# A two-layer decoder trunk in float32: the second score matmul of attention branches A and B over 128 rows instead of 64

## The chip, the core and the metric

The kernel runs on one core of a Trainium2 chip. The metric is the device time of one execution in microseconds (us). Engines are named as in the profile: PE is TensorE's matmul, PEld its weight load, DVE is VectorE, ACT is ScalarE, POOL is GpSimd, SP is SyncE.

## What is computed

Two layers of a decoder trunk on 512 tokens of width 1024. Per layer, h = RMSNorm(x), one input projection feeds three causal mixers, their outputs are gated and merged, then follow an output projection with a residual and a SwiGLU FFN with another. Branch A has 8 heads of width 64, branch B has 4 heads with two score maps each (differential attention), branch C has 8 heads of width 96 for the scores. The part that matters here:

```
scores of A: sc = q @ k.T * 64**-0.5 + bias_a[distance]        # q, k: 512 x 64 per head
scores of B: sc_i = q_i @ k_i.T * 64**-0.5 + bias_b[distance]  # i = 0, 1
p = softmax(masked sc)
```

## The kernel before

**Float32 by parts.** Every operand of a product is split into a hi part (rounded to fp32r) and a lo part (what is left), and a product is hi\*hi + hi\*lo + lo\*hi, three fp32r matmuls into one PSUM bank (`mm3`, line 264). The dense work (projections, gates, FFN) streams weights in units of up to 128x512: SP loads them, ACT makes the hi part (`_hi`, line 221), DVE the lo part (`_lo`, line 227).

**Scores of A and B.** Rows of a tile are SBUF partitions. `q_tile` (line 639) and `k_tile` (line 653) each turn one projection tile of 128 rows, two heads of 64 rows, into operands. For q, each head gets one tile that holds its hi part in its own 64 rows and its lo part in the other 64. For k, each head gets a tile with its hi part in both row halves (ACT writes one half at line 659, POOL copies it to the other at line 663), and both heads share a third tile, `k[2]`, with the lo parts, one in each half (DVE, line 662). `qk_stacked` (line 667) then makes one block of scores from two matmuls into one PSUM bank: the first runs over all 128 rows (hi of q and lo of q against hi of k), the second over the 64 rows of the head (hi of q against lo of k). A block is 128 queries by n keys, where n = 128, 256, 384, 512 for the four query blocks. A layer has 16 such score maps (8 heads of A, two for each of 4 heads of B), so 64 blocks, and the two layers have 128 such pairs of matmuls. Branch C uses `qk_plain` (line 675): three matmuls over 96 rows per block.

**Behind the scores.** `score_block` (line 693) adds the bias and takes the row maximum on DVE and the exponential on ACT; `scale_rows` (line 704) normalizes the rows on POOL; `transposed` (line 709) transposes the blocks on PE, and ACT and DVE split them for the product with v.

**Order.** The program is issued in a fixed order, in which each engine takes its own instructions one after the other. `weave` (line 363) makes that order: up to three threads of attention pieces (heads) run, and between them come steps of dense jobs. It decides by `Clock` (line 86), a rough model of every engine's time, in which a matmul costs by its columns alone (line 99) and a POOL operation on 512 columns about 0.66 us (line 105). A piece is issued when its inputs are ready by that model, else a dense step is. The k tiles of A and B are dense jobs (`qk_jobs`, line 680): in a layer the first tile of A stands ahead of the attention, the others among the jobs (lines 1074 to 1104). There are 16 k tiles in the two layers. All tiles of 128x512 come from one pool of 83 slots (`NSLOT`, line 30).

Of the kernel before, what the change touches and what calls it, by code (L numbers as in the profile page):

```python
# [9 lines left out]
F32 = mybir.dt.float32  # L10
F32R = mybir.dt.float32r
AF = mybir.ActivationFunctionType
ALU = mybir.AluOpType
# [5 lines left out]
P = 128  # L19
# [66 lines left out]
class Clock:  # L86
    """A rough clock of the engines while the program is traced. It only decides the order in
    which independent pieces are issued; Tile places every wait."""
    HOP = 0.18
# [74 lines left out]
class Kernel:  # L164
# [11 lines left out]

# [1 line left out]
    def slot(self, dt=F32):  # L178
# [23 lines left out]

# [1 line left out]
    def add_job(self, units, body, ready=None):  # L204
# [41 lines left out]
    def ahead(self, i, most=2):  # L246
        """loads and splits up to unit i and, a few at a time, beyond it"""
        n = len(self.units)
        ld, lh, ll = self.look
        self.load_ahead(min(n, i + 1 + ld))  # L250
        end = min(n, i + 1 + lh, max(i + 1, self.ph + most))
        while self.ph < end:
            self._hi(self.ph)
            self.ph += 1
        end = min(n, i + 1 + ll, max(i + 1, self.pl + most))
        while self.pl < end:
            self._lo(self.pl)
            self.pl += 1
# [3 lines left out]

# [1 line left out]
    def mm3(self, out, ah, al, bh, bl, first, last):  # L264
# [4 lines left out]

    def t_job(self, tiles, per_unit=4, halves=False, ready=None):  # L270
        """tiles: (wname, layer, [k-blocks], cols, rhs() -> [(hi, lo)], evac(psum));
        W block stationary, activations moving."""
        blocks = [(t, kb) for t in range(len(tiles)) for kb in range(len(tiles[t][2]))]
# [46 lines left out]
    def n_job(self, wname, layer, ks, cols, lhs, evac, groups=None, ready=None):  # L320
        """activations' token block stationary, W columns moving; evac(tb, psum)."""
        w = len(cols)
        units = [[(wname, layer, k, cols)] for k in ks]
        groups = groups or [1] * len(ks)

        def body(j):
            ps = None
            k0 = 0
            for g in groups:
                for tb in range(NT):  # L330
                    if g > 1 or tb == 0:
                        self.ahead(j.base + k0 + g - 1, 3)
                    if k0 == 0:
                        if ps is None:
                            ps = [None] * NT
                        ps[tb] = self.bank()
                    for kb in range(k0, k0 + g):
                        h, l = self.hi[j.base + kb], self.lo[j.base + kb]
                        ah, al = lhs(kb, tb)
                        o = ps[tb][:, :w]  # L340
                        mm = self.nc.tensor.matmul
                        mm(o, ah, h[:, :w], start=kb == 0, stop=False)
                        mm(o, ah, l[:, :w], start=False, stop=False)
                        mm(o, al, h[:, :w], start=False, stop=kb == len(ks) - 1)
                        if g > 1 and kb == k0 + g // 2 - 1:
                            yield
                    if k0 + g == len(ks):
                        evac(tb, ps[tb])
                    if g > 1 or tb == 1:
                        yield  # L350
                for kb in range(k0, k0 + g):
                    self.done(j.base + kb)
                k0 += g
                if g == 1:
                    yield

        return self.add_job(units, body, ready)
# [5 lines left out]
    def weave(self, threads, jobs):  # L363
        """Issues the threads' pieces as they come ready and dense steps in between.
        threads: list of (generator of readiness functions, group); a readiness function
        gives the time at which its piece can start, or None while that is unknown."""
        clock, free = self.clock, self.clock.free
# [41 lines left out]

# [1 line left out]
    def split(self, hi, lo, src, scale=None):  # L411
# [11 lines left out]

# [1 line left out]
    def rstd(self, parts):  # L425
        """parts: [P,1] shares of the mean square; -> (mean + eps) ** -0.5"""
        nc = self.nc
# [8 lines left out]
    def sumsq(self, src, out, n):  # L436
        """out = sum(src ** 2) / n"""
        self.nc.scalar.activation(self.junk[:, :src.shape[-1]], src, AF.Square, scale=n ** -0.5, accum_out=out)
# [10 lines left out]
    def norm_block(self, x, ss, g):  # L449
        """x: two halves of a token block -> normed halves (F32)."""  # L450
        nc = self.nc
# [46 lines left out]
def program(K):  # L498
# [26 lines left out]

# [1 line left out]
    bias_in = (K.slot(F32), [K.slot(F32) for _ in range(2)], [K.slot(F32) for _ in range(2)])  # L527
# [44 lines left out]
    def setup_bias():  # L572
        """bias of every distance, per head, and from it 128 rows to cut the strips from"""
        tab, oh, us = bias_in
# [23 lines left out]
def layer(K, l, plan, state, strip, C):  # L598
# [4 lines left out]

# [1 line left out]
    def norm1_stats(tb):  # L605
# [13 lines left out]

# [1 line left out]
    def v_evac(key, heads, hd):  # L621
        """token-major values as [hi | lo] per head, two slots per token block"""
        res = [None] * NT
# [13 lines left out]

# [1 line left out]
    def q_tile(key, off, m):  # L639
        """two heads of 64 rows; each gets one tile that stacks its hi and lo parts"""  # L640
        def evac(ps):
# [11 lines left out]
    def k_tile(key, off, m):  # L653
        """hi parts doubled over both row halves, lo parts of the two heads in one tile"""
        def evac(ps):
            k = [K.slot(F32R) for _ in range(3)]
            for i in range(2):
                a = slice(i * 64, i * 64 + 64)
                nc.scalar.copy(k[i][a], ps[a])
            for i in range(2):  # L660
                a, b = slice(i * 64, i * 64 + 64), slice(64 - i * 64, 128 - i * 64)
                nc.vector.tensor_tensor(k[2][a], ps[a], k[i][a], op=ALU.subtract)
                nc.gpsimd.tensor_scalar(k[i][b], k[i][a].bitcast(F32), 1.0, 1.0, op0=ALU.mult, op1=ALU.mult)
            V[key, m] = k
        return ("w_in", l, range(KD), rng(off + m * P, P), h, evac)

    def qk_stacked(q, k, i):
        rows = slice(i * 64, i * 64 + 64)

        def mm(out, qs, n):  # L670
            nc.tensor.matmul(out, q[i][:, qs], k[i][:, :n], start=True, stop=False)
            nc.tensor.matmul(out, q[i][rows, qs], k[2][rows, :n], start=False, stop=True)
        return mm
# [8 lines left out]

# [1 line left out]
    def when(keys, tiles, banks=0):  # L684
        """the time at which a piece can start; None before its inputs are issued"""
        def at():
# [22 lines left out]
    def transposed(ps):  # L709
        """P blocks -> per key block the (hi, lo) parts of its columns, queries from that block on"""  # L710
        pt = {}
# [19 lines left out]
    def head(hd, start, vkey, ykey, y):  # L731
        """one head of A or C: y[pair] collects the transposed outputs of two heads"""
        mm, ins, bias = yield from start(hd)
# [31 lines left out]

# [1 line left out]
    def start_a(hd):  # L767
# [5 lines left out]

# [1 line left out]
    def low_rank_evac(key, gi, w):  # L775
# [6 lines left out]
    def low_rank_q():  # L782
        """norm of cq and its transpose"""
        g = [K.slot(F32), K.slot(F32)]
# [24 lines left out]
    def low_rank_kv():  # L809
        """norm of ckv and its transpose; the rotary key, transposed"""  # L810
        g = K.slot(F32)
# [87 lines left out]

# [1 line left out]
    def head_b(hd, y):  # L901
# [65 lines left out]

# [1 line left out]
    BR = {"a": 0, "b": 1, "c": 2}  # L969
# [24 lines left out]

# [1 line left out]
    def residual_evac(hf, g_key):  # L996
# [17 lines left out]

# [1 line left out]
    V["ff"], V["m"] = {}, {}  # L1016
# [30 lines left out]

    # ======== jobs, in the order in which the tensor engine takes them ========
    def given(keys, tiles=lambda: []):
# [25 lines left out]
    jobs = []  # L1075
# [35 lines left out]
    def reload():  # L1111
        """the residual stream and the gain of the next norm"""
        src = ap["x"] if l == 0 else x_dram
# [20 lines left out]

    # ======== program ========
    def drain(jobs):
# [111 lines left out]
```

## Time and profile before

| | |
|---|---|
| three runs | 1924.22, 1925.93, 1927.16 us; median 1925.93 us |
| the profiled execution | known by its span, from the first to the last instruction: 1922.5 us, 3.4 us under the median |
| PE busy | 1895.5 us, 99% of the span |
| PEld, DVE, ACT, POOL busy | 82%, 48%, 42%, 12% |
| granted TensorE clock | 0.999 of full speed in the mean |

In the rows further down, a matmul or a weight load carries the rows and columns of the stationary operand and then the moving operand: `64*128 64x512` has 64 rows, 128 stationary columns and 512 moving columns. A timeline row merges neighbours of one kind and shows the first one's form. A matmul's own duration contains its way through the pipeline, so neighbours overlap; what a matmul takes of the engine is read from its start to the start of the next row. `<-issue` means that the engine waited for nothing that the profile shows.

### The profile page before, as it was taken

How to read it: one execution, taken by the hardware profiler on the slowest of the kernel's cores; microseconds unless marked ns; L12 is line 12 of the kernel's file. 1: busy time of each engine (PE TensorE's matmuls, PEld its weight loads, DVE VectorE, ACT ScalarE, POOL GpSimd, SP SyncE). 2: the span in 40 equal slices, each digit the busy share in tenths (PEclk: the TensorE clock that was granted, in tenths of full speed). 3: DMA queues.
4: the chain of work that ended last, by engine and by line, in shares of the span. 5: the costliest groups of instructions: out<-in, count | busy, mean ns of one | idle time of the engine just before them, and what ended most of it. 6: DMA issues, size and time to landing. Idle time of an engine off the chain costs nothing.

```text
span 1922.5 us, 25100 instructions
## 1 busy us (share of the span) xinstructions
PE 1895.5 (99%) x9148; PEld 1581.0 (82%) x9148; DVE 915.1 (48%) x1836; ACT 800.9 (42%) x1777; POOL 223.8 (12%) x405
## 2 busy tenths in 40 slices
PE   7999999999999999999999999999999999999998
PEld 5798988777888888888888888887878898888886
DVE  4556556556465333342354566565563553323331
ACT  4456655454344222232235656554443432323330
POOL 3222412111000000000002233211110000000000
PEclk9999999999999999999999999999999999999999
DMA  7422223224343322232423222132333332222321
GB/s 264 103 82 64 72 77 94 76 73 128 108 126 100 88 77 83 83 115 83 148 94 95 61 75 71 58 110 74 120 105 99 126 94 82 83 77 85 119 93 44
DMA packets 104604, 183.05 MB, mean 95 GB/s; under 512 B 13888, under 2 KB 24576, under 8 KB 104480
## 3 DMA queue, kind: packets, MB, share of 16 engines
q1 hardware_dynamic: 99216, 173.91, 29.4%
q0 software_dynamic: 3824, 4.91, 0.9%
q10 hardware_dynamic: 1440, 2.62, 0.4%
q8 instruction: 72, 1.18, 0.2%
q14 instruction: 52, 0.43, 0.1%
HBM read 177.15 MB, written 8.16 MB: 96 GB/s over the span
## 4 chain that ended last, share of the span: by engine, by line
PE 95%; DVE 2%; DMA 2%; ACT 1%; issue 0%; DVEq 0%; POOLq 0%; POOL 0%; ACTq 0%
PE d L154 83%; PE a L154 12%; DVE s L154 2%; ACT s L154 1%; DMA s<-in_x 1%; DMA s<-in_weights 1%; DMA s<-in_lambda_k 0%; DVEq L1237 0%; ACT junk L154 0%; DVE h L154 0%; POOLq L1237 0%; DVE gsub L154 0%; POOL m L154 0%; DVE lam L154 0%; DVE junk L154 0%
## 5 line engine op out<-in xcount | busy, mean ns | idle before, releaser
L154 PE MATMUL d<-h,s 128*128 128x512 f32 (+1 forms) x4224 | 947.8, 382 | 1.3 <-DVE s L154 1.3
L154 PEld LDWEIGHTS d<-h,s 128*128 128x128 f32 x4224 | 761.3, 188 | 151.3 <-issue 3.3
L154 PE MATMUL d<-s,s 128*128 128x512 f32 (+1 forms) x2400 | 548.3, 385 | 1.8 <-DVE s L154 1.8
L154 DVE TENSOR_TENSOR s<-s,s 128x512 fp32r<-128x512 f32 (+3 forms) x718 | 451.9, 669 | 184.1 <-ACT s L154 130.0
L154 PEld LDWEIGHTS d<-s,s 128*128 128x128 f32 x2400 | 443.3, 188 | 86.4 <-issue 3.6
L154 ACT CAST s<-s 128x512 fp32r<-128x512 f32 (+2 forms) x678 | 378.3, 603 | 278.0 <-DVE s L154 212.7
L154 PE MATMUL d<-s,h 128*128 128x512 f32 (+2 forms) x960 | 200.7, 358 | 7.7 <-DVE s L154 6.0
L154 PE MATMUL a<-s,s 128*128 128x256 f32 (+8 forms) x868 | 188.7, 332 | 8.9 <-DMA s<-in_c_onehot 8.9
L154 PEld LDWEIGHTS d<-s,h 128*128 128x128 f32 x960 | 162.9, 189 | 30.7 <-issue 8.8
L154 PEld LDWEIGHTS a<-s,s 128*128 128x128 f32 (+2 forms) x868 | 140.7, 188 | 53.7 <-issue 25.2
L154 DVE TENSOR_TENSOR s<-a,s 128x512 fp32r<-128x512 f32 (+5 forms) x196 | 111.5, 606 | 143.2 <-ACT s L154 142.6
L154 ACT ACTIVATE s<-s,m 128x128 f32<-128x128 f32 x192 | 107.7, 561 | 133.9 <-DVE m L154 132.3
L154 DVE TENSOR_TENSOR s<-d,s 64x512 fp32r<-64x512 f32 (+2 forms) x128 | 72.1, 587 | 170.6 <-PE d L154 110.7
L154 POOL TENSOR_SCALAR m<-m 128x1 f32<-128x1 f32 (+1 forms) x44 | 16.0, 363 | 1132.9 <-ACT junk L154 1132.7
L154 POOL TENSOR_SCALAR s<-s,m 128x128 f32<-128x128 f32 (+3 forms) x160 | 97.2, 625 | 426.9 <-DVE m L154 266.8
L154 DVE TENSOR_TENSOR s<-s,d 128x512 f32<-128x512 f32 x44 | 30.3, 688 | 226.8 <-PE d L154 226.8
L154 ACT ACTIVATE junk<-s 128x512 f32<-128x512 f32 (+3 forms) x96 | 47.0, 490 | 173.0 <-DVE s L154 167.2
L154 ACT ACTIVATE s<-d 128x512 f32<-128x512 f32 (+1 forms) x76 | 45.3, 596 | 148.4 <-PE d L154 148.2
L154 PE MATMUL a<-ident,s 128*128 128x128 f32 (+1 forms) x696 | 95.6, 278 | 0.0
L154 ACT CAST s<-a 128x512 fp32r<-128x512 f32 (+2 forms) x146 | 69.7, 534 | 59.8 <-PE a L154 59.1
L154 DVE CUSTOM_DVE_ANT_0 s<-a,s 128x128 f32<-128x128 f32 (+3 forms) x128 | 60.8, 489 | 68.5 <-PE a L154 68.1
L154 DVE SCALAR_TENSOR_TENSOR s<-s,m,s 128x512 f32<-128x512 f32 (+3 forms) x96 | 64.8, 713 | 58.3 <-POOL m L154 46.5
(48 smaller groups left out, 575.4 us busy)
## 6 DMA issues: line engine op xcount, KB each, us to landing
s<-in_weights SPq DMA_DIRECT2D x542, 256.0 KB, 2.7
s<-in_weights SPq DMA_DIRECT2D x56, 192.0 KB, 2.6
s<-u_rep SPq DMA_DIRECT2D x24, 256.0 KB, 2.7
s<-in_x SPq DMA_DIRECT2D x16, 256.0 KB, 5.9
s<-in_weights SPq DMA_DIRECT2D x16, 144.0 KB, 2.1
x_dram<-s ACTq DMA_DIRECT2D x8, 256.0 KB, 3.4
s<-x_dram SPq DMA_DIRECT2D x8, 256.0 KB, 5.4
out<-s SPq DMA_DIRECT2D x8, 256.0 KB, 2.0
```

The costliest lines, as they stand in the source:

```text
L154: return f(*args, **kw)
```

## The change

`k_tile` makes four tiles instead of three: the lo parts no longer share one tile, each head gets its own, in both row halves. The second half is a copy by POOL of what DVE wrote, two more POOL operations of 64x512 for each k tile, issued behind the two that copy the hi parts. The second matmul of a block runs over all 128 rows: the stationary operand is the same as that of the first (hi and lo of q), the moving operand is the doubled lo part of k. The block thereby also gets the product lo\*lo, which was left out before. The rest of the diff removes comments and docstrings.

```
     def k_tile(key, off, m):
         def evac(ps):
-            k = [K.slot(F32R) for _ in range(3)]
+            k = [K.slot(F32R) for _ in range(4)]
             for i in range(2):
                 a = slice(i * 64, i * 64 + 64)
                 nc.scalar.copy(k[i][a], ps[a])
             for i in range(2):
                 a, b = slice(i * 64, i * 64 + 64), slice(64 - i * 64, 128 - i * 64)
-                nc.vector.tensor_tensor(k[2][a], ps[a], k[i][a], op=ALU.subtract)
+                nc.vector.tensor_tensor(k[2 + i][a], ps[a], k[i][a], op=ALU.subtract)
                 nc.gpsimd.tensor_scalar(k[i][b], k[i][a].bitcast(F32), 1.0, 1.0, op0=ALU.mult, op1=ALU.mult)
+            for i in range(2):
+                a, b = slice(i * 64, i * 64 + 64), slice(64 - i * 64, 128 - i * 64)
+                nc.gpsimd.tensor_scalar(k[2 + i][b], k[2 + i][a].bitcast(F32), 1.0, 1.0, op0=ALU.mult, op1=ALU.mult)
             V[key, m] = k
...
     def qk_stacked(q, k, i):
-        rows = slice(i * 64, i * 64 + 64)
-
         def mm(out, qs, n):
             nc.tensor.matmul(out, q[i][:, qs], k[i][:, :n], start=True, stop=False)
-            nc.tensor.matmul(out, q[i][rows, qs], k[2][rows, :n], start=False, stop=True)
+            nc.tensor.matmul(out, q[i][:, qs], k[2 + i][:, :n], start=False, stop=True)
         return mm
```

## Rows read from the trace of the kernel before

**Rows 1.** The page, busy us of each engine (share of the span) and its instructions.
```profile
PE 1895.5 (99%) x9148; PEld 1581.0 (82%) x9148; DVE 915.1 (48%) x1836; ACT 800.9 (42%) x1777; POOL 223.8 (12%) x405
```

**Rows 2.** Busy by stretch, layer 0: A's later heads, then C's. Columns as its header.
```profile
core 0: us, PE busy (x) PEld busy (x) DVE busy (x) ACT busy (x) POOL busy (x), PEclk, DMA share, GB/s
...
143.00:188.00 45.00, 44.65 (x243) 36.71 (x244) 28.96 (x85) 27.13 (x72) 9.27 (x18) 1.00 0.23 65
188.00:339.00 151.00, 151.00 (x810) 132.41 (x809) 88.09 (x199) 87.28 (x197) 47.51 (x90) 1.00 0.26 81
```

**Rows 3.** Groups by form, PEld: busy, mean ns, then idle before them and its end.
```profile
L154 PEld LDWEIGHTS a<-s,s 96*128 96x128 f32 x192 | 31.3, 189 | 4.1
L154 PEld LDWEIGHTS a<-s,s 64*128 64x128 f32 x128 | 23.5, 184 | 26.2 <-issue 21.2 <-DVE s L154 0.4
```

**Rows 4.** Timeline of PE, layer 0, B's first head: start us, us, line, operation.
```profile
345.31 0.59 PE L154 MATMUL a<-s,s 128*128 128x256 f32 x2
345.83 1.66 PE L154 MATMUL d<-s,h 128*128 128x512 f32 x6
347.33 0.70 PE L154 MATMUL a<-s,s 128*128 128x384 f32 x2
347.96 1.66 PE L154 MATMUL d<-s,h 128*128 128x512 f32 x6
349.45 0.82 PE L154 MATMUL a<-s,s 128*128 128x512 f32 x2
350.20 2.12 PE L154 MATMUL d<-s,h 128*128 128x512 f32 x8
```

**Rows 5.** Timeline of PE, layer 0, one block of 128 columns of A.
```profile
81.64 0.48 PE L154 MATMUL a<-s,s 128*128 128x128 f32 x2
82.05 1.31 PE L154 MATMUL d<-s,h 128*128 128x384 f32 x6
```

**Rows 6.** Timeline of PE, layer 1, four blocks of B directly behind one another.
```profile
1403.32 2.69 PE L154 MATMUL a<-s,s 128*128 128x128 f32 x8
1405.95 1.66 PE L154 MATMUL d<-h,s 128*128 128x512 f32 x6
```

**Rows 7.** Timeline of PE, layer 0, blocks of C: three matmuls over 96 rows each.
```profile
227.27 0.86 PE L154 MATMUL a<-s,s 96*128 96x512 f32 x3
227.96 1.52 PE L154 MATMUL d<-h,s 128*128 128x512 f32 x6
...
236.10 0.69 PE L154 MATMUL a<-s,s 96*128 96x384 f32 x3
236.62 1.54 PE L154 MATMUL d<-h,s 128*128 128x512 f32 x6
...
254.52 0.45 PE L154 MATMUL a<-s,s 96*128 96x128 f32 x3
254.81 1.61 PE L154 MATMUL d<-h,s 128*128 128x512 f32 x6
256.26 0.52 PE L154 MATMUL a<-s,s 96*128 96x256 f32 x3
256.62 1.56 PE L154 MATMUL d<-h,s 128*128 128x512 f32 x6
```

**Rows 8.** Timeline, layer 0: making the first k tile of A, and its first scores.
```profile
55.69 1.32 POOL L154 TENSOR_SCALAR s<-s 64x512 fp32r<-64x512 f32 x2 [0.87 <-PE d L154]
56.17 1.41 DVE L154 TENSOR_TENSOR s<-d,s 64x512 fp32r<-64x512 f32 x2 [2.72 <-ACT s L154]
...
58.83 2.69 PE L154 MATMUL a<-s,s 128*128 128x128 f32 x8
```

**Rows 9.** Timeline, layer 0, PE's waits behind A's first heads; brackets: idle before, its end.
```profile
62.82 0.23 DVE L154 CUSTOM_DVE_ANT_0 junk<-s 128x64 f32<-128x64 f32 x1 [1.71 <-DMA s<-in_lambda_k]
...
64.86 2.56 PE L154 MATMUL d<-h,s 128*128 128x512 f32 x10 [1.28 <-DVE s L154]
...
76.51 0.76 PE L154 MATMUL d<-s,h 128*128 128x384 f32 x3 [2.85 <-DVE s L154]
```

**Rows 10.** Groups by form, POOL: the copies of hi parts; columns as in rows 3.
```profile
L154 POOL TENSOR_SCALAR s<-s 64x512 fp32r<-64x512 f32 x32 | 19.7, 616 | 87.9 <-ACT s L154 61.1 <-issue 14.2 <-PE a L154 10.4
```

More of the change, by code (lines that the diff above doesn't have):

```diff
@@ L655, in evac @@
         def evac(ps):
-            k = [K.slot(F32R) for _ in range(3)]
+            k = [K.slot(F32R) for _ in range(4)]
             for i in range(2):
@@ L661, in evac @@
                 a, b = slice(i * 64, i * 64 + 64), slice(64 - i * 64, 128 - i * 64)
-                nc.vector.tensor_tensor(k[2][a], ps[a], k[i][a], op=ALU.subtract)
+                nc.vector.tensor_tensor(k[2 + i][a], ps[a], k[i][a], op=ALU.subtract)
                 nc.gpsimd.tensor_scalar(k[i][b], k[i][a].bitcast(F32), 1.0, 1.0, op0=ALU.mult, op1=ALU.mult)
+            for i in range(2):
+                a, b = slice(i * 64, i * 64 + 64), slice(64 - i * 64, 128 - i * 64)
+                nc.gpsimd.tensor_scalar(k[2 + i][b], k[2 + i][a].bitcast(F32), 1.0, 1.0, op0=ALU.mult, op1=ALU.mult)
             V[key, m] = k
@@ L667, in qk_stacked @@
     def qk_stacked(q, k, i):
-        rows = slice(i * 64, i * 64 + 64)
         def mm(out, qs, n):
             nc.tensor.matmul(out, q[i][:, qs], k[i][:, :n], start=True, stop=False)
-            nc.tensor.matmul(out, q[i][rows, qs], k[2][rows, :n], start=False, stop=True)
+            nc.tensor.matmul(out, q[i][:, qs], k[2 + i][:, :n], start=False, stop=True)
         return mm
```

## The prediction

> **What bounds the kernel now.** I read the busy shares first. TensorE's matmul row is busy 99% of the span, the next compute engine 48% [rows 1]. A busy PE is not PE at its peak, so the question is how much of those 99% the touched matmuls hold without need.
>
> For that I went to the weight loads by form. 128 loads of 64 rows stand there, one for each second matmul of a score block in A and B, and ahead of them the load path sat idle 26.2 us, 21.2 of it for nothing that the profile shows. The 192 loads of 96 rows in branch C, which do the same kind of work, have 4.1 us [rows 3]. So a 64-row load is kept waiting, while its operand, the same q tile as that of the first matmul, is long there.
>
> The timeline of PE prices it. I take from the start of a pair to the start of what comes next. Standing alone between dense steps, a pair takes 0.52 us at 256 columns, 0.63 at 384 and 0.75 at 512 [rows 4], and 0.41 at 128 [rows 5]: 2.31 us for the four blocks of a map. Branch C is the comparison: there three matmuls over 96 rows, between the same dense steps, take 0.69 us at 512, 0.52 at 384, 0.36 at 256 and 0.29 at 128 [rows 7]. Two matmuls of A cost more than three of C. A switch between 128 rows and 64 rows, once into it and once out of it, is the one thing that A and B have and C lacks; 96 rows beside 128 cost nothing that is seen.
>
> Last I read the stretches, to see whether another engine would take over. In A's later stretch DVE is busy 28.96 of 45 us and ACT 27.13; in C's, where no such switch slows PE, DVE has 88.09 of 151 and ACT 87.28, and PE is busy without a break [rows 2]. At the pace without switches the other engines keep up.
>
> **The change, part by part.**
>
> *The second matmul over 128 rows.* It gets the form of its neighbours, so both switches of all 128 pairs go. Its price without them comes from C: a third of a block, 0.23, 0.173, 0.12 and 0.097 us [rows 7], so a pair costs two thirds: 0.46 + 0.35 + 0.24 + 0.19 = 1.24 us for four blocks. More rows add no columns, and 96 and 128 rows are both above the 64, so I take C's price as it stands. Against 2.31 us that saves 1.07 us per map; 32 maps give 34.2 us.
>
> That is the sum for pairs that stand alone. Pairs directly behind one another cost more: four of them take 2.63 us [rows 6], 0.32 over 2.31, so 0.107 for each of the three that follow another. In the timeline 52 of the 128 pairs follow another pair in this way (19 at 256 columns, 13 at 384, 13 at 512, 7 at 128). 52 x 0.107 = 5.6 us. Together **39.8 us** off PE. Bounds: 34.2 if only the stand-alone price goes, and 44.5 (32 x (2.63 - 1.24)) if all pairs cost as in rows 6.
>
> *What does not arrive.* Where PE waits for something that PE's pace doesn't move, the gain before it is lost. After the first heads of layer 0, PE waits 1.28 us and then 2.85 us for DVE [rows 9]. DVE's work there had been held up until 62.82 by the transfer of the lambdas [rows 9], which no matmul delays, and from there DVE and ACT follow one another closely. So what is won in the seven pairs ahead of the second wait only lengthens the waits: the first four, 2.63 - 1.24 = 1.39 us, and one each at 128, 256 and 384 columns, 1.56 us [rows 4, 5] and 0.1 for the one that follows another, less 0.78, 0.9 us. Together 2.3 us. I take that off: 37.5 us. In layer 1, the wait at the same place hangs on ACT's copy of a projection that PE itself ends, so it moves along; nothing is taken off there. Bounds: 0 to 4.6 (the same in both layers).
>
> *Two more POOL copies for each k tile.* 16 tiles x 2 x 0.616 us [rows 10] = 19.7 us on an engine that is busy 223.8 of 1922.5 us [rows 1]. The tightest place is the first head, whose scores start right behind its k tile: POOL's hi copies end at 57.01, DVE's two lo parts at about 56.88 and 57.58, and the first score starts at 58.83 [rows 8]. The new copies would run from 57.01 to 57.63 and from 57.58 to 58.20, 0.6 us ahead of the first score, and the second head, which uses the last copy, comes later. So they hide; without that cover, PE would wait 0.6 us or so at one tile. On POOL's queue, the scaling of an older head's rows may now stand behind two copies, 1.23 us; the order is planned with POOL's time in it, which puts a dense step in front of the transposes that wait. I take 0, bounds -1 to +10 us (half of 19.7).
>
> *DVE, ACT, DMA.* DVE writes the same two lo parts, to two tiles instead of one; counts and sizes stay. Nothing moves on SP. One more slot per k tile: counted from the code in issue order, at most 67 of the 83 slots are live while A and B make scores, and one or two more change nothing. 0 us.
>
> *The order.* `Clock` prices a matmul by its columns, so the plan's PE doesn't change, but two more POOL operations shift readiness times, and a few pieces will change places. PE's idle time behind the first 30 us is about 7 us, in eight gaps, of which rows 9 show the largest two. A changed plan can lose or add that much: 0, bounds -5 to +7.
>
> **The sum.** The span is 1922.5 us and the median of the runs 1925.93, 3.4 above; I keep that distance. 1922.5 - 37.5 + 3.4 = 1888.4 us. I predict **1888 us**, 2.0% under before.
>
> **The rivals.**
>
> *The load still waits.* What rows show: dense and 96-row loads run ahead of their matmuls without a wait, 64-row loads don't [rows 3]. Suppose instead that a load must wait wherever the previous matmul uses the same rows: then in the new pairs, which share all 128 rows, the second load would still stand behind the first matmul, and pairs would cost what they do now: 1926 us. Against it speaks rows 7, where three loads on the same 96 rows cost 0.23 us per 512-column matmul. This is also the case in which the change doesn't do what it says.
> The Trainium skill states such a rule (TensorE: Matmul & The Clock Gate, Part 3, The mechanism): a weight load overlaps a matmul in flight only where the row groups differ. By that rule nothing would be won; the trace disagrees, by the same rows 7 (0.23 us for each of three matmuls on the same rows).
>
> *Another engine takes a share.* A's heads run three at a time beside splits for projections; DVE is at 64% there [rows 2]. If half of A's share (64 of 128 pairs, 19.9 us) is lost in new waits for DVE, ACT or POOL, it is 1898 us; if all of it is, 1908. For it: PE already waits for DVE twice at A's start [rows 9]. Against it: C's stretch.
>
> *Slower: POOL becomes the way to the scores.* The copies of lo parts wait at the head of POOL's queue for DVE's subtractions. If at each of the 16 k tiles PE stood through both, 1.41 us for DVE's pair [rows 8] and 1.23 for two copies, that is 2.64 us a tile, 42 us in all: 1930 us. It decides from 37.5 / 16 = 2.35 us a tile. Against it: rows 8 leave some 0.6 us even at the tightest tile, and the other tiles are made long before their heads begin.
>
> **How the numbers follow.** The forecast as worked out (1881 to 1896) gets 0.84, another engine's share 0.09, the load that still waits 0.03, slower by POOL 0.04. The range is 1881 to 1899: below, the sum with 44.5 us and a plan that loses some waits; above, POOL's 10 us, or half of A's share gone. That leaves out the longer half of the second rival and the last two, and some of the forecast's own edges, between 1 and 2 in 10. A measurement of this kernel tells about 0.2% (3.9 us) from no change; faster 0.93, same 0.03, slower 0.04.
>
> **What would show it.** Right: no 64-row form is left in the groups; a stand-alone pair takes 0.46 us at 512 columns and 0.19 at 128; four in a row 1.24 and not 2.63; the loads of these blocks have the small idle time of the 96-row ones; PE's busy time falls by 38 to 40 us; the wait near 76 us in layer 0 grows by up to 2.3 us; POOL's busy time grows by about 20 us. Wrong: pairs that still take 0.7 us at 512 columns (the first rival), or pairs at 0.46 with new waits of PE for POOL or DVE around the heads (the others).

## The result, and the profile after

The changed kernel takes 1874.07 us (1873.35 to 1875.83, 4 runs), the kernel before 1925.08 beside it: a ratio of 0.9738, interval 0.9724 to 0.9752, so 51.0 us or 2.6% less. The prediction was 1888 us with a range of 1881 to 1899: the right way and the right mechanism, but the gain came out at 1.36 times what was forecast, and the time 7 us below the range.

The page of the changed kernel, busy time of each engine, against rows 1:

```profile
PE 1847.8 (99%) x9148; PEld 1576.4 (84%) x9148; DVE 915.8 (49%) x1836; ACT 794.7 (42%) x1777; POOL 248.2 (13%) x437
```

PE has as many instructions as before and is busy 47.7 us less; the span fell by 50.6, from 1922.5 to 1871.9. DVE and ACT do what they did. POOL has 32 instructions and 24.4 us more, which nobody waits for, as will be seen.

The weight loads by form, changed kernel (busy, mean ns, idle before), against rows 3:

```profile
L154 PEld LDWEIGHTS a<-s,s 128*128 128x128 f32 x672 | 103.4, 189 | 8.9
L154 PEld LDWEIGHTS a<-s,s 96*128 96x128 f32 x192 | 31.3, 189 | 4.1
```

No 64-row form is left. The 128 loads that sat behind 26.2 us of idle time are now among 672 that have 8.9 us together. C's row is the same to the digit.

The timeline of PE in the same head as rows 4, changed kernel:

```profile
330.43 0.51 PE L154 MATMUL a<-s,s 128*128 128x384 f32 x2
330.78 1.54 PE L154 MATMUL d<-s,h 128*128 128x512 f32 x6
332.16 0.62 PE L154 MATMUL a<-s,s 128*128 128x512 f32 x2
332.61 8.33 PE L154 MATMUL d<-s,h 128*128 128x512 f32 x36
```

From start to start, the pair at 512 columns takes 0.45 us (0.75 before, 0.46 forecast) and that at 384 columns 0.35 (0.63, and 0.35). Now look one row further, where the prediction did not: the six dense matmuls behind a pair take 330.78 to 332.16, 1.38 us. In rows 4 the same six take 347.96 to 349.45, 1.49, and the ones before them 345.83 to 347.33, 1.50. Something like 0.11 us of the switch lies behind the pair, in the dense matmuls.

Adding up the intervals between the starts of all matmuls in the two traces, with PE's idle time apart: the 256 matmuls of the pairs take 40.4 us less (39.8 forecast), all other matmuls 7.3 us less, and PE's idle time in between is 3.3 us shorter. That is the span's 50.6 us but for 0.4 at its two ends. So the prediction was exact on what it priced, and missed some 10 us beside it. Two theories were put to the test. **Theory 1:** a 64-row matmul costs three intervals of PE: the one in front of it, its own, and one more behind it; with 0.107 us for each of the 128 pairs, and not only for the 52 that follow another, rows 4 to 7 give 34.2 + 13.7 = 48 us. **Theory 2:** a switch costs what was counted, and the rest came from the new order in which the pieces are issued.

### The profile page after: what moved, and what is told of

Same layout as the page of the kernel before. It is cut to its first block, busy times and chain, and to the rows that moved or that the text cites. A ratio compares the mean times of both kernels' runs of the same rounds, so it can differ in the third digit from the quotient of the medians.

```text
span 1871.9 us, 25152 instructions
## 1 busy us (share of the span) xinstructions
PE 1847.8 (99%) x9148; PEld 1576.4 (84%) x9148; DVE 915.8 (49%) x1836; ACT 794.7 (42%) x1777; POOL 248.2 (13%) x437
## 4 chain that ended last, share of the span: by engine, by line
PE 95%; DVE 2%; DMA 1%; ACT 1%; issue 0%; SPq 0%; DVEq 0%; POOLq 0%; POOL 0%; ACTq 0%
PE d L154 85%; PE a L154 11%; DVE s L154 2%; ACT s L154 1%; DMA s<-in_weights 0%; DMA s<-in_lambda_k 0%; DMA s<-in_x 0%; DMA s<-u_rep 0%; SPq L154 0%; DVEq L1238 0%; ACT junk L154 0%; POOLq L1238 0%; DVE gsub L154 0%; POOL m L154 0%; DVE lam L154 0%
## 5 line engine op out<-in xcount | busy, mean ns | idle before, releaser
L154 PE MATMUL a<-s,s 128*128 128x256 f32 (+8 forms) x868 | 154.7, 313 | 9.1 <-DMA s<-in_c_onehot 9.1
L154 PEld LDWEIGHTS a<-s,s 128*128 128x128 f32 (+2 forms) x868 | 134.9, 188 | 22.9 <-DMA s<-in_rel_bias_table 9.1
L154 PEld LDWEIGHTS a<-ident,s 128*128 128x128 f32 (+1 forms) x696 | 81.2, 140 | 11.1 <-DVE s L154 1.5
```

What stands on the lines that cost most here:

```text
L154: return f(*args, **kw)
```

## The experiments

### The same order, 64 rows again

The changed kernel with all its tiles and copies; only the second matmul reads half of them. The order on every engine is that of the changed kernel.

```
+        rows = slice(i * 64, i * 64 + 64)
...
-            nc.tensor.matmul(out, q[i][:, qs], k[2 + i][:, :n], start=False, stop=True)
+            nc.tensor.matmul(out, q[i][rows, qs], k[2 + i][rows, :n], start=False, stop=True)
```

> The changed kernel with all it prepares (four k tiles, the two more copies, the order of every engine), but the second matmul reads only the 64 rows of its head again. Theory 1: a 64-row matmul costs three intervals of PE, entering it, leaving it and the one behind that, whose successor's load is late too; rows of before give 34.2 us for stand-alone pairs and 0.107 us for each of the 128 pairs, 48 us in all. Then this kernel takes 1874 + 48 = 1922 us, and dense matmuls of 512 columns behind a pair take about 0.34 us, not 0.23. Theory 2: a pair costs only what the prediction counted (39.8 us), and the rest of the gain came from the new order: 1914 us.

Measured: 1923.5 us (1918.94 to 1924.98), ratio to before 0.9989, interval 0.9979 to 0.9999. That is 49.4 us over the changed kernel, with one slice as the only difference: nearer to theory 1's 48 than to theory 2's 40. The median holds a second effect, though: six of the ten runs have a granted clock of 0.996 and take 1923.2 to 1925.0 us; the other four, the traced one among them, have 0.998 and take 1918.9 to 1920.5. So the time alone leaves some 4 us open. The two traces settle it, since they hold the same matmuls in the same order: from start to start, the 256 matmuls of the pairs take 40.2 us more than in the changed kernel, the 74 that stand directly behind a pair without being one 7.3 us more (0.098 each), and everything else, waits included, 1.2 us less. Theory 1 has both parts. Its timeline of PE, B's first head:

```profile
342.24 0.71 PE L154 MATMUL a<-s,s 128*128 128x384 f32 x2
342.88 1.63 PE L154 MATMUL d<-s,h 128*128 128x512 f32 x6
344.35 0.81 PE L154 MATMUL a<-s,s 128*128 128x512 f32 x2
345.09 3.25 PE L154 MATMUL d<-s,h 128*128 128x512 f32 x13
```

The pairs are back at 0.64 and 0.74 us, and the six dense matmuls behind one at 1.47.

The weight loads show it. The kernel before, in the stretch of rows 4:

```profile
347.59 0.18 PEld L154 LDWEIGHTS a<-s,s 64*128 64x128 f32 x1 [0.30 <-issue]
347.96 1.23 PEld L154 LDWEIGHTS d<-s,h 128*128 128x128 f32 x6 [0.19 <-issue]
```

In the changed kernel's trace a load starts 3 or 4 ns behind the start of the matmul ahead of its own, and runs beside it. Here the 64-row load starts only when its own matmul does (347.59), and so does the load of the first dense matmul behind the pair (347.96). The load after that, inside the row of six, starts 0.107 us behind the start of the first dense matmul, so the second one follows after 0.335 us and not 0.227. That is the third interval.

### The old order, 128 rows, no copies

The kernel before with one edit; the order on every engine is that of before, and no instruction is added. The sums of this kernel and of those made from it contain lo of q times lo of the other head's k, which the scores don't have.

```
-            nc.tensor.matmul(out, q[i][rows, qs], k[2][rows, :n], start=False, stop=True)
+            nc.tensor.matmul(out, q[i][:, qs], k[2][:, :n], start=False, stop=True)
```

> The kernel before, with one edit: the second matmul runs over 128 rows against the lo tile that both heads share, so no copies, no fourth tile, and the order of every engine is that of before. (It thereby adds lo of q times lo of the other head's k, which is no part of the scores.) Theory 1: 48 us less than before on PE, and the first waits of layer 0 grow by what was won ahead of them (2 to 3 us): 1925 - 48 + 2.5 = 1879.5 us; the changed kernel's other 5 us would then be its new order at the start of the attention. Theory 2: 1925 - 39.8 + 2.3 = 1887.5 us.

Measured: 1878.77 us (1878.28 to 1879.64), ratio 0.9762, interval 0.9748 to 0.9777: 45.7 us less than before. Theory 1 gave 1879.5, theory 2 1887.5. Matmul by matmul against the kernel before, in the same order: the pairs' intervals are 40.1 us shorter, those of the 76 matmuls directly behind a pair, 74 of them dense, 7.25 us (0.095 each), and everything else, waits included, 1.8 us longer. Its timeline, DVE and PE, against rows 9:

```profile
62.66 0.23 DVE L154 CUSTOM_DVE_ANT_0 junk<-s 128x64 f32<-128x64 f32 x1 [0.80 <-DMA s<-in_lambda_k]
...
64.69 2.57 PE L154 MATMUL d<-h,s 128*128 128x512 f32 x10 [1.49 <-DVE s L154]
...
76.33 1.30 PE L154 MATMUL d<-s,h 128*128 128x384 f32 x3 [3.48 <-DVE s L154]
```

DVE is held until 62.66 (62.82 before), and the wait ends at 76.33 (76.51 before): by then nearly all that the first seven pairs had won was gone again. Only some 1.1 us of it went into longer waits (5.2 us in all, 4.1 before). Another 1.1 us went already at the start, where this run's clock came up to full later, at 24.9 us and not at 19.1: matched by their place in the order, its dense matmuls run 1.1 us behind those of before until the attention begins. This kernel stays 4.7 us above the changed one. That is left for the order, or for the copies.

### Order and copies apart

Two kernels cross what the change joins. In the first (made from the one above) the copies are only told to the rough clock that makes the order; in the second (the changed kernel) they are issued and not told.

```
+                K.clock.note("gpsimd", "tensor_scalar", k[2][b], [k[2][a]], [])
```
```
-                nc.gpsimd.tensor_scalar(k[2 + i][b], ...)
+                nc.gpsimd.eng.tensor_scalar(k[2 + i][b], ...)
```

> The kernel with 128 rows and no copies (e2_no_copies), but its order is made as if the copies were there, so every engine has the order of the changed kernel, POOL just lacks the 32 copies. The changed kernel is 4.7 us under e2_no_copies. If the new order is what gives these 4.7 us: 1874 us, and PE's waits for DVE near 63 and 73 us are short (together under 2 us, not 5). If it is something about the copies or the separate lo tiles: 1879 us.

> The changed kernel with its copies and tiles, but its order is made as if the copies were not there, so every engine has the order of before. If the copies hide, as the prediction said, and only the order matters: 1879 us, as e2_no_copies, and PE has no wait for POOL. If the copies cost: more than 1880 us, with waits of PE for POOL at the first scores of a head. If the order gives nothing: 1874 us.

Measured:

| 128 rows | order of before | order of the changed kernel |
|---|---|---|
| no copies | 1878.77 | 1874.07 (1873.90 to 1874.74) |
| 32 copies | 1879.24 (1878.79 to 1880.14) | 1874.07 |

The ratios are 0.9743 (0.973 to 0.9757) with the new order and no copies, and 0.9771 (0.9757 to 0.9784) with the old order and the copies. The copies cost nothing that can be measured, in either order; the order alone gives some 5 us. So each theory holds a part of what the prediction missed: the third interval, and the order. One expectation failed narrowly: with the new order and no copies PE's two waits were to stay under 2 us together, and are 1.72 and 0.73. Why the copies hide shows in the tightest place, the first head in the kernel with the old order and the copies (timeline, POOL and PE):

```profile
58.34 1.31 POOL L666 TENSOR_SCALAR s<-s 64x512 fp32r<-64x512 f32 x2
...
60.09 1.43 PE L154 MATMUL a<-s,s 128*128 128x128 f32 x8
```

The copies end at 59.65, 0.44 us ahead of the first score; the prediction had 0.6.

What the new order does is seen in the timeline of the changed kernel, PE, the start of the attention in layer 0:

```profile
51.74 9.68 PE L154 MATMUL d<-h,s 128*128 128x512 f32 x42
61.27 0.97 PE L154 MATMUL a<-s,s 128*128 128x128 f32 x6
62.08 0.63 PE L154 MATMUL d<-h,s 128*128 128x512 f32 x2
63.39 1.20 PE L154 MATMUL d<-h,s 128*128 128x512 f32 x4 [0.69 <-DVE s L154]
...
73.13 2.84 PE L154 MATMUL d<-s,h 128*128 128x384 f32 x15 [1.10 <-DVE s L154]
```

Since the model has the k tile ready later, it puts more dense steps ahead of the first score, and the pieces behind it fall differently. PE's two waits for DVE are 0.69 and 1.10 us here, against 1.28 and 2.85 in the kernel before [rows 9] and 1.49 and 3.48 in the old order with 128 rows.

### What held DVE

The prediction took the transfer of the lambdas (four small rows of parameters a layer, for branch B) for the cause of these waits. In two kernels the lambdas are loaded at the very start through ACT's queue, with the order unchanged: one from the kernel with the old order, 128 rows and no copies, the other from the changed kernel.

```
+    for l in range(DEPTH):
+        for i in range(4):
+            nc.scalar.eng.dma_start(lv[l][:, i * 64:i * 64 + 64], lam_row(l, i))
...
-                K.bcast_row(lv[l][:, i * 64:i * 64 + 64], ap[n][l], nc.gpsimd)
+                K.clock.note("gpsimd", "dma_start", lv[l][:, i * 64:i * 64 + 64], [lam_row(l, i)], [])
```

> As e2_no_copies (128 rows, no copies, the order of before), but the lambdas are loaded at the start through ACT's queue, so DVE need not wait for them. If that transfer holds DVE, and so eats what PE wins ahead of 76 us, as the prediction said: PE's waits near 63 and 76 us, together 5.2 us in e2_no_copies, fall under 2.5 us, and the time falls by 2 to 4 us, to 1875 to 1877. If DVE and ACT are simply late there: the waits stay at about 5 us, and the time at 1879.

> The changed kernel with the lambdas loaded at the start in the same way. Its waits at that place are 0.7 and 1.1 us. If they come from the lambdas too: about 1 us less, 1873 us, not to be told from 1874; if not: the same.

Measured: 1886.39 us (1885.30 to 1887.81), ratio 0.9808 (0.9794 to 0.9821), and 1884.26 (1883.44 to 1884.75), ratio 0.9796 (0.9782 to 0.9809). Both expectations failed: the kernels are 7.6 and 10.2 us slower than those they were made from, where 2 to 4 and 1 us less had been expected, or at worst no change. PE's longest waits in the first of the two say where:

```profile
23.20 1.97 PE L154 MATMUL a<-ident,s 128*128 128x128 f32 x8 [12.04 <-DVE s L154]
...
84.52 0.77 PE L154 MATMUL d<-s,h 128*128 128x384 f32 x3 [2.58 <-DVE s L154]
```

The first transposes wait 12 us. ACT has the eight loads ahead of its first squares; its queue issues them between 13.43 and 18.50 us, and the squares start at 19.82 instead of 5.17. What held the first of these loads until 13.43 the trace does not show. The delay is the experiment's own doing. Behind it the kernel catches up: matched by their place in the order, its dense matmuls run 11.3 us behind those of its parent at the end of the first projections and 6.4 at 180 us. One of the two waits is gone, the other 2.58 and not 3.48. So the load was moved again, to SP, at the place in the order where POOL had it:

```
-                K.bcast_row(lv[l][:, i * 64:i * 64 + 64], ap[n][l], nc.gpsimd)
+                K.clock.note("gpsimd", "dma_start", lv[l][:, i * 64:i * 64 + 64], [src], [])
+                nc.sync.eng.dma_start(lv[l][:, i * 64:i * 64 + 64], src)
```

> As e7_early_lambda, but the lambdas are loaded by SP, at the place in the order where POOL loaded them, so ACT's work at the start is not held up (there the first transposes came 12 us late). e7's stretch from the end of the first value projection to 180 us was 4.9 us shorter than that of e2_no_copies. If that is the held-back gain: 1878.8 - 4.9, so about 1874 us, as much as the new order gives, and PE's waits near 63 and 73 us together under 3 us. If it was only the later start: 1879 us.

Measured: 1873.91 us (1872.98 to 1874.80), ratio 0.9738 (0.9724 to 0.9751), so 4.9 us less than with POOL's loads, as expected. PE's only wait in this stretch:

```profile
71.99 0.77 PE L154 MATMUL d<-s,h 128*128 128x384 f32 x3 [2.56 <-DVE s L154]
```

The lambdas' transfer did hold DVE, and through it PE. Two ways around it, other dense steps in between or the load through another queue, are worth the same 5 us. In what remains (2.56 us) DVE waits for no transfer by this trace, only for ACT. Not all of the gain is wait. In the attention's first stretch PE waits 2.6 us less than with POOL's loads (5.2, the sum of the waits there, against 2.56); by their places in the order its dense matmuls gain 4.7 us in that stretch, and most of the other 2 us are matmuls that had run at half clock behind the long wait (some 1.5 us between 76 and 80 us). The busy times by stretch (columns as in rows 2; the granted clock is the number behind POOL's), first the kernel with POOL's loads, then this one:

```profile
75.00:82.00 7.00, 5.67 (x28) 5.52 (x29) 4.43 (x9) 2.09 (x5) 0.90 (x2) 0.76 0.22 66
```
```profile
75.00:82.00 7.00, 7.00 (x45) 6.83 (x44) 5.02 (x21) 4.50 (x14) 2.55 (x4) 1.00 0.32 101
```

After a wait of 3.48 us the clock stands between its two levels of 1.2 and 2.4 GHz in the mean, 0.76; after one of 2.56 us at full. The kernel before has 0.76 in this stretch, the changed kernel 1.00. So part of the difference between these traces is a clock that did not fall. It is not the length of the wait alone that decides: in the new order without copies the clock fell behind a wait of 1.72 us (0.83 from 60 to 70 us), and that run's span is still 1872.9 us, against 1877.0 in the old order.

The changed kernel with the same load by SP was run as well, as the one that might beat both:

> The changed kernel with the lambdas loaded by SP as in e9_sp_lambda: does it beat the changed kernel? Its waits for DVE near 63 and 72 us are 0.7 and 1.1 us. If the lambdas make them, about 1 us less: 1873 us, too little to be told from 1874. If they don't, the same.

Measured: 1871.85 us (1871.65 to 1873.09), ratio 0.9728, interval 0.9714 to 0.9741. It is the lowest time of all, 2.2 us under the changed kernel's median, but the intervals of the two ratios overlap (0.9724 to 0.9752): an advantage that these runs cannot establish.

### Switch or form

Is it the switch that costs, or a 64-row matmul as such? Three kernels make two score blocks in one piece of a head: 128, 64, 128, 64 rows; 128, 128, 64, 64; and 128 throughout.

```
+            for out, qs, n in blocks:
+                nc.tensor.matmul(out, q[i][:, qs], k[i][:, :n], start=True, stop=False)
+            for out, qs, n in blocks:
+                nc.tensor.matmul(out, q[i][rows, qs], k[2 + i][rows, :n], start=False, stop=True)
```

> As the first kernel (64 rows), but a piece of a head makes two score blocks: 128 rows, 64, 128, 64. As many switches as before, all pairs of a piece directly behind one another. Both theories: near 1922 us, give or take 5 for another order of pieces. It is the measure for the next one.

> The same pieces of two blocks, but 128, 128, 64, 64: as many 64-row matmuls, half as many switches. If the switch is what costs: half of 48 us less than by turns, about 24 us, so near 1898. If each 64-row matmul is slow by itself, whatever stands beside it: the same as by turns.

> As e4a_by_turns, in the same order on every engine, but the second matmul over 128 rows. Switches by theory 1: 48 us less than by turns, plus some 10 us for the stretches in which the clock stood at half in that kernel (30.7 us at half in its records): 1936 - 58 = 1878 us, with no half-clock stretch behind the first 100 us. The grouped kernel should then stand in the middle of what the switches alone cost: 1878 + 24 = 1902 us, as it does.

Measured: by turns 1935.94 us (1930.46 to 1936.42), grouped 1902.61 (1901.80 to 1903.71), all over 128 rows 1879.61 (1878.69 to 1880.81); ratios to before 1.0044 (1.0026 to 1.0062), 0.9886 (0.9871 to 0.9901) and 0.9767 (0.9754 to 0.9781). By turns missed its expectation (1922, give or take 5) by 14 us, and grouped, expected near 1898 from there, came out 4.6 us above; over 128 rows met its 1878. Grouped and by turns have the same 128 matmuls of 64 rows. Grouped, with half of the switches, costs 23.0 us over the kernel without any, half of 48 within 1 us. It is the switch. One piece of two blocks (128 and 256 columns) in B's first head, then the dense matmuls behind it, grouped:

```profile
337.59 0.81 PE L154 MATMUL a<-s,s 128*128 128x128 f32 x4
338.34 1.66 PE L154 MATMUL d<-s,h 128*128 128x512 f32 x6
```

and by turns:

```profile
345.13 1.09 PE L154 MATMUL a<-s,s 128*128 128x128 f32 x4
346.15 1.66 PE L154 MATMUL d<-s,h 128*128 128x512 f32 x6
```

0.75 us against 1.02 for the same four matmuls.

By turns costs 56.3 us over 128 rows, 8 more than the switches explain. The rest goes with the clock: the two runs with a granted clock of 0.995 take 1930.5 us, the three with 0.991 take 1935.9 to 1936.4. Two stretches of the trace show it, by turns and then over 128 rows:

```profile
455.00:480.00 25.00, 25.00 (x83) 17.95 (x83) 13.00 (x33) 10.09 (x26) 3.71 (x6) 0.80 0.16 50
1330.00:1355.00 25.00, 25.00 (x84) 17.78 (x83) 14.88 (x37) 11.04 (x27) 5.65 (x8) 0.80 0.25 75
```
```profile
455.00:480.00 25.00, 25.00 (x124) 21.03 (x123) 15.57 (x28) 8.72 (x22) 1.27 (x2) 1.00 0.47 152
1330.00:1355.00 25.00, 25.00 (x129) 21.26 (x127) 15.81 (x36) 14.08 (x39) 3.56 (x6) 1.00 0.51 160
```

## Why the prediction was right and wrong, point by point

**What bounds the kernel: right.** PE was the path. What PE no longer did came off the time: 50.6 us of span for 51.0 us of intervals and waits.

**The second matmul over 128 rows: right in kind, one term short.** Both switches are gone, C's price holds (0.45 and 0.35 us a pair against 0.46 and 0.35), and the pairs' own intervals shrank by 40.4 us where 39.8 were forecast. The step that failed is the one that charged 0.107 us "for each of the three that follow another" and nothing for the other 76 pairs. The extra was taken for a price of pairs in a row. It is the third interval of every switch: what stands behind a 64-row matmul has its successor's load late, whether that is a score or a dense matmul. For a pair in a row it fell into the next pair's sum and was seen; for the 76 others it lay in the matmul behind, nearly always a dense one, outside the interval that was measured. 76 x 0.107 would be 8.1 us. The old order with 128 rows, where nothing else changed, shows it: the 76 matmuls directly behind a pair take 7.25 us less there, 0.095 each. Rows 4 held it, with six dense matmuls at 1.50 us; the comparison with six behind a block of C was not made.

**What does not arrive: right in kind, mis-sized.** In the old order what the first pairs won was gone at the waits that the lambdas' transfer sets; loading them through SP gave it back, and some more with the clock. But the waits there grew by 1.1 us and not by 2.3; another 1.1 us is the later start of that one run. In the changed kernel's order they are 0.53 us with 64 rows and 1.79 with 128, and in layer 1, where nothing was taken off, 0.36 and 1.33: 2.2 us together. That loss is hidden in the result, since the new order made all of these waits shorter in the first place.

**POOL's copies: right.** 0 us in both orders, with 0.44 us to spare at the tightest tile where 0.6 were forecast. (The sum let the second copy start 0.05 us before the first ended, which changes nothing.)

**The order: mis-sized.** It was taken as 0 with bounds of -5 and +7. The new order gave about 5 us, the edge of its bound, and made the very waits shorter at which 2.3 us had been written off. The prediction did look at the largest gaps, and expected the order to move pieces; it could have said that the first scores move behind more dense steps exactly where PE waited.

With the two terms as measured the sum nearly closes: 1888.4 - 7.25 - 4.9 = 1876.2 us. Of the last 2.1 us, 1.2 are the distance from span to median, 2.2 us in this kernel and not 3.4; 0.9 stay open.

**The rivals.** A load that waits wherever the rows are shared is refuted: pairs that share all 128 rows run at 0.45 us. Another engine took no share beyond that: PE's waits are 3.3 us shorter than before. POOL is not in the way.

**The range** had the bound of 44.5 us on the switch and the bound of -5 on the order, but not both together, and the first was too low: it let "all pairs" cost as rows 6, where one pair's third interval still lies outside.

## What to carry to other kernels

In this kernel a stream of matmuls over 128 rows pays about 0.37 us for every excursion to 64 rows and back (47.3 us for 128 of them). If the other half of the rows can be filled with something true or harmless, that time comes back whole, as long as PE is the path; if the excursions are grouped in twos, half of it. When a disturbance is priced from a timeline, go on measuring until the intervals are those of an undisturbed stretch again: here one interval too few hid about a sixth of the effect. And where the order is planned by a model, a new instruction can matter through the plan alone; issuing it without telling the model, and telling without issuing, takes the two apart.

## What the runs showed of the hardware that was not expected

A 64-row matmul between 128-row ones disturbs the matmul behind the one that follows it, by about 0.1 us (six dense matmuls at 1.49 us instead of 1.38; 0.095 us in the mean of 76).

TensorE's clock fell to its lower level while PE was busy without a break. By turns, the records show half clock in several stretches of layer 0 and 1, 30.7 us in all, with PE busy 25.00 of 25 us in the two stretches above. The same form takes 1.57 us in an earlier head at full clock and 2.58 at half (timeline of PE, by turns):

```profile
342.14 1.57 PE L154 MATMUL a<-s,s 128*128 128x384 f32 x4
...
460.69 4.22 PE L154 MATMUL a<-s,s 128*128 128x128 f32 x12
464.84 2.93 PE L154 MATMUL d<-h,s 128*128 128x512 f32 x6
467.57 2.58 PE L154 MATMUL a<-s,s 128*128 128x384 f32 x4
470.08 2.93 PE L154 MATMUL d<-h,s 128*128 128x512 f32 x6
```

At 460.69 the clock falls within a run of twelve matmuls of alternating rows directly behind one another, and each of the other three falls stands in or right behind such a run too. Over 128 rows in the same order, and grouped in nearly the same, it did not happen. PE's busy time is the same in both. The changed kernel's order with 64 rows has one such stretch as well, behind five pairs in a row (granted clock 0.72 from 1400 to 1406 us, PE busy 6.00 of 6 us). The kernel before differs from run to run in step with its clock: over all experiments 1921.4 to 1923.8 us where 0.999 was granted, 1927.4 to 1927.8 where it was 0.995. So a few of the 51.0 us at the top may be clock and not switch; where it fell in those runs no trace shows. What exactly the clock answers to was not tried further.
